# Hybrid decoder block: block sums and norm scales on one engine, another order of seven block products

## The chip, the cores and the metric

The kernel runs on one core of one Trainium2 chip. The time is the device time of one execution in microseconds (us). Of several executions the median counts. The engines are TensorE (PE; its weight loads are PEld), VectorE (DVE), ScalarE (ACT), GpSimd (POOL) and SyncE (SP). SP and POOL also start DMAs; each does what it is given in order.

## The reference

One decoder block, 1024 tokens, width 1024, float32. The part around the change, cut:

```
h = rms_norm(x, norm1_g)
z = h @ w_in                      # (1024, 3352 + 2048): q 512 | kv 768 | gates 24 | retention 2048 | merge 2048
q = rms_norm(zq per head of 64) * nsa_q_norm              # 8 heads
k_slc, k_win = rms_norm(k per head of 64) * nsa_k_norm[1], [2]     # 2 groups each
v_slc, v_win                                              # as they are
y_nsa = gates * (compressed, selected, sliding-window attention over q, k, v)
y_ret = silu(g) * group_norm(retention(q, k, v))
x = x + (sigmoid(zm) * (y_nsa @ w_b0, y_ret @ w_b1)).sum() @ w_out
x = x + (silu(rms_norm(x) @ w_gate) * (rms_norm(x) @ w_up)) @ w_down
```

## The kernel before

A float32 product is made of three fp32r products: each operand is split into a high part (a ScalarE copy to fp32r) and a low part (a VectorE subtraction). The normed input lies transposed in `H` as such a pair.

The kernel is written as generators that yield operations (`Op`), allocations (`Alloc`) and waits on flags (`Wait`). A planner, `Sched`, picks the next operation by costs of its own, and the order of picking is the order on each engine. `Any` gives it two engines to choose from, one VectorE, one GpSimd. A `Ring` or `Bag` is a set of buffers. What the planner's time says is not what the chip does; the chip waits on semaphores, each engine in its own order.

The change lies in the stage between the input norm and the retention projections, some 50 to 220 us into the span. It computes the 512 columns of q and 512 columns of k and v (branches 1 and 2) for all tokens as a 2 by 2 block product with seven multiplications instead of eight. Tokens 0 to 511 and 512 to 1023 are the two row blocks, the two halves of the width are the inner blocks, q and kv the column blocks.

- `g_sums` makes the sums of activation blocks out of `H` (11 VectorE subtractions and additions for each of four k), splits two of them into `gSa` and `gSb`, and stores two others in `s_scr`, which `s_back` loads back later and splits into `gSa` and `gSb` when products 6 and 7 have read these. Its scratch tiles come from `gt_ring`, three tiles of 128x512 (later five).
- The weight blocks are loaded into `R[0]` to `R[3]` by `b_loads`, 128x512 for each k. `R[1]` and `R[3]` serve other ends before that (compressed keys, gate values).
- `qk_sums` makes the sums of weight blocks in place in `R` and in tiles of `gt_ring`; `sub` lets the planner choose VectorE or GpSimd.
- `qk_ops` and `qk_fill` split each weight operand into one of six `oq` tiles, in the order of `QSEQ`.
- `qk_main` is the TensorE side: for each product p and token tile t, 12 matmuls (4 k, 3 parts). Products 1, 6, 7 and 4 add up in four banks (psS, psO); 2, 5 and 3 take a psF bank each. `qk_post` reads them out: product 2 gives q tiles 0 to 3, product 5 gives k/v tiles 4 to 7, product 3 k/v tiles 0 to 3, product 4 q tiles 4 to 7.
- `q_tile` and `kv_tile` norm a tile: square (ACT), sum (DVE), power −1/2 (POOL, `rsq`), scale (DVE), multiplication by `gq` or `gk` (POOL), split into `cat` (ACT, DVE), transposes (PE, psT), copy to a tile of `gt_ring` (ACT), DMA to `q_scr`, `k_scr`, `v_scr`. There are two `cat` tiles.
- `g_main` follows with the retention projections by the same seven-product scheme: products (1,0), (2,0), (1,1), (2,1) need only `H` and raw weights, then come those with `gRS` (sums from `sp_scr`, loaded by POOL's DMA into the space of `R`), whose weight sums (`gTab`) take the space of `cat`.

L316 is the matmul, L320 and L321 transposes, L336 a ScalarE copy, L346 a VectorE or GpSimd two-operand operation, L365 the sum, L386 and L387 the two GpSimd steps of `rsq`, L369 a DMA from POOL, L370 one from SP.

Of the kernel before, what the change touches and what calls it, by code (L numbers as in the profile page):

```python
# [9 lines left out]
F32 = mybir.dt.float32  # L10
# [250 lines left out]
def kernel(  # L261
# [144 lines left out]
        return bass.AP(tensor=ap.tensor, offset=ap.offset, ap=[[0, 128], [1, n]])  # L406

    q_scr = [[dram.tile([192, 512], F32, name=f"q_scr{g}_{t}") for t in range(NT)] for g in range(2)]
    k_scr = [dram.tile([128, 2, T], F32, name=f"k_scr{br}") for br in range(2)]
    v_scr = [dram.tile([128, 2, NT, 128], F32, name=f"v_scr{br}") for br in range(2)]  # L410
    r_scr = [[dram.tile([128, T], F32, name=f"r_scr{h}_{i}") for i in range(4)] for h in range(4)]
    s_scr = [dram.tile([128, 4, 512], F32, name=f"s_scr{i}") for i in range(2)]
    sp_scr = [dram.tile([128, 2, 4, 512], F32, name=f"sp_scr{i}") for i in range(2)]
# [120 lines left out]
    def a_loads():  # L534
        yield from x_load(0)
        yield dma(grow, norm1_g)
        for kk in range(4):
            yield from w_load(kk)
            if kk == 1:
                yield from x_load(1)  # L540
        yield dma(rawZ, w_cols(G0, 0, 8, 24))
        sch.spawn(a_wsplit(whA[:, 0, :, 256:280], whA[:, 1, :, 256:280], rawZ, 4), 3)
        for t in range(2, NT):
            yield from x_load(t)
        for i in range(3):
            yield dma(gk[:, i, :], bcast_rows(nsa_k_norm[0, i], HD))
        yield dma(q1, bcast_rows(nsa_q_norm[0], HD))
        yield Op("dve", 70, 60, [zpad], [], lambda: dve.memset(zpad, 0.0))
        yield dma(c_scr[:, :, T:T + 16, :].rearrange("a g t d -> t (a g) d"), zpad)
        yield from load_units(z_units[:2])  # L550
        yield from cw_loads()
        yield Wait(lambda: all(("xn", t) in fl for t in range(NT)))
        sch.spawn(split_units(z_units), 3)
        yield from load_units(z_units[2:3])
        yield Wait(lambda: ("cX", 1) in fl)
        yield from load_units(z_units[3:])
        for m, k in ((0, 0), (2, 1), (1, 2)):
            yield Wait(lambda: ("ss", 1, k) in fl)
            yield from b_loads((m,))
        yield Wait(lambda: "plain" in fl)  # L560
        yield from b_loads((3,))
        for j, S in ((2, gSa), (3, gSb)):
            for k in range(4):
                yield Wait(lambda: ("gS", j, k) in fl)
                yield dma(sp_scr[j - 2][:, :, k], S[:, :, k].bitcast(F32))
# [167 lines left out]
    def q_tile(t, z, free):  # L733
        zv = z.rearrange("p (h d) -> p h d", d=HD)
        own = yield Alloc(gt_ring)
        qn = own.rearrange("p (h d) -> p h d", d=HD)
        yield from q_norm(zv, qn, qn)
        free()
        yield tt(qn, qn, qk["gq"], ALU.mult, gp)
        cat = yield Alloc(qk["cat"])  # L740
        yield from split(cat[:, :, 0:64], cat[:, :, 64:128], qn)
        gt_ring.release(own)
        for g in range(2):
            tp = yield Alloc(t_ring)
# [12 lines left out]
    def kv_tile(t, z, free):
        zv = z.rearrange("p (b c n) -> p b c n", b=2, c=2)
        kz, vz = [zv[:, :, i].rearrange("p b (g d) -> p b g d", g=2) for i in range(2)]
        vs = yield Alloc(gt_ring)  # L760
        vw = vs.bitcast(F32R).rearrange("p (b g n) -> p b g n", b=2, g=2)
        yield from split(vw[:, :, :, 0:64], vw[:, :, :, 64:128], vz)
        for b in range(2):
            yield dma(v_scr[b][:, :, t, :], vs[:, b * 256:b * 256 + 256].rearrange("p (g n) -> p g n", g=2))
        gt_ring.release(vs)
        yield from q_norm(kz, vz, kz)
        yield tt(kz, kz, gk[:, 1:3, None, :].to_broadcast([128, 2, 2, HD]), ALU.mult, gp)
        cat = yield Alloc(qk["cat"])
        cv = cat[:, 0:4].rearrange("p (b g) n -> p b g n", b=2)
        yield from split(cv[:, :, :, 0:64], cv[:, :, :, 64:128], kz)  # L770
        free()
        tp = yield Alloc(t_ring)
        for j in range(4):
            yield tr(tp[:, j * 128:(j + 1) * 128], cat[:, j, :])
        qk["cat"].release(cat)
        ks = yield Alloc(gt_ring)
        yield ac(ks.bitcast(F32R), tp)
        t_ring.release(tp)
        for b in range(2):
            yield dma(k_scr[b][:, :, t * 128:(t + 1) * 128], ks[:, b * 256:b * 256 + 256].rearrange("p (g n) -> p g n", g=2))  # L780
            fl.add(("kv", b, t))
        gt_ring.release(ks)
        fl.add(("post", "k", t))

# [57 lines left out]
    gps = ExitStack()  # L842
    gtp, gpr, gpq = [gps.enter_context(tc.tile_pool(name=n, bufs=1, side="right")) for n in ("gtp", "gpr", "gpq")]
    gm, gops, gT1, gT2, gT4, gt, qk = {}, {}, {}, {}, {}, {}, {}
    gt_ring = Bag([gtp.tile([128, 512], F32, name=f"gt{n}") for n in range(3)])
    gSb = gpr.tile([128, 2, 4, 512], F32R, name="gSb")
    gSa = gpq.tile([128, 2, 4, 512], F32R, name="gSa")
    cp = ExitStack()
# [48 lines left out]
    def g_sums():  # L897
        yield Wait(lambda: ("cX", 1) in fl)
        def w(v):
            return v.rearrange("p (t n) -> p t n", t=4)  # L900

        def put(j, k, v):
            S = gSa if j == 2 else gSb
            yield from split(S[:, 0, k], S[:, 1, k], v)
            fl.add(("gS", j, k))

        for k in range(4):
            def h(i, j, p):
                return H[:, p, 4 * i:4 * i + 4, 4 * j + k, :].bitcast(F32)
            a = yield Alloc(gt_ring)  # L910
            yield tt(w(a), h(1, 0, 0), h(1, 1, 0), ALU.add)
            t = yield Alloc(gt_ring)
            yield tt(w(t), h(1, 0, 1), h(1, 1, 1), ALU.add)
            yield tt(a, a, t, ALU.add)
            yield tt(w(t), w(a), h(0, 0, 0), ALU.subtract)
            yield dma(s_scr[0][:, k], a, lat=2000)
            fl.add(("ss", 0, k))
            gt_ring.release(a)
            yield tt(w(t), w(t), h(0, 0, 1), ALU.subtract)
            yield from put(2, k, t)  # L920
            s = yield Alloc(gt_ring)
            yield tt(w(s), h(1, 1, 0), w(t), ALU.subtract)
            yield tt(w(s), w(s), h(1, 1, 1), ALU.add)
            yield from put(3, k, s)
            gt_ring.release(s)
            yield tt(w(t), h(0, 1, 0), w(t), ALU.subtract)
            yield tt(w(t), w(t), h(0, 1, 1), ALU.add)
            yield dma(s_scr[1][:, k], t, lat=2000)
            fl.add(("ss", 1, k))
            gt_ring.release(t)  # L930
        fl.add("gS0")

    def s_back():
# [11 lines left out]
        for t in raws:  # L945
            raw_ring.release(t)
        fl.add("back")
        for j, b, after in ((2, 1, 7), (2, 0, 5), (3, 1, 3), (3, 0, 4)):
            yield Wait(lambda: all((after, k) in q_ops for k in range(4)))
            S = gm["S", j, b] = gl.tile([128, 4, 512], F32R, name="gRS", tag=f"r{j * 2 - 4 + b}")  # L950
            yield dma(S, sp_scr[j - 2][:, b], gp)

    QSEQ = (1, 2, 6, 7, 5, 3, 4)
    q_ops = {}

    def qk_ops():
# [22 lines left out]
    def qk_sums(odd):  # L979
# [115 lines left out]
    def g_loads():  # L1095
        yield Wait(lambda: "back" in fl)
        gm["raw"] = [(yield Alloc(raw_ring)), (yield Alloc(raw_ring))]
        for j, (n, f) in enumerate(g_todo):
            if j == 2:
                yield Wait(lambda: ("P", 4) in fl)  # L1100
                gm["raw"] += [gpl.tile([128, 8, 128], F32, name="xx", tag=f"o{i}") for i in (2, 3)]
            h, i = r_pairs[f]
            t = yield Alloc(graw_ring)
            yield dma(t, r_units[h][i + (n == "U")].src)
            gm[n, f] = t
# [16 lines left out]
    def g_ops():  # L1122
        gm["h"] = []
        made = set()
        for n, (p, f) in enumerate(gseq):
            yield Wait(lambda: ("G", f) in gm)
            G = gm["G", f]
            if n < 4:
                yield Wait(lambda: all((4, k) in q_ops for k in range(4)) and (4, 5, 0, 1)[n] not in qk["op"].held)
            if n in (4, 6):  # L1130
                yield Wait(lambda: "wh" in fl)
                gm["h"].append((yield Alloc(hl_ring)))
# [72 lines left out]
        gop_ring.release(w)  # L1205

    def g_main():
        yield Wait(lambda: "plain" in fl and ("P", 4) in fl)
        Y, Z = {}, {}
        for p, f in gseq:  # L1210
            yield Wait(lambda: (p, f) in gops and (p not in (6, 7) or all(("S", p - 4, b) in gm for b in range(2))))
# [477 lines left out]
    def load_group(g):  # L1689
        yield Wait(lambda: us[0] in qt)  # L1690
        for br in (1, 0):
            kT[br].append(kvp.tile([128, T], F32R, name=f"kT{br}"))
            vv[br].append(kvp.tile([128, NT, 128], F32R, name=f"vv{br}"))
            yield dma(kT[br][g], k_scr[br][:, g], gp, 3000)
            yield dma(vv[br][g], v_scr[br][:, g], gp, 3000)
            fl.add("kv1")
        fl.add(("gkv", g))

# [816 lines left out]
```

## Time and profile before

| | us |
|---|---|
| median of 3 runs | 1583.86 |
| lowest, highest | 1582.41, 1584.09 |
| profiled execution | 1583.02 |
| its span | 1581.2 |
| TensorE busy | 1544.2 |
| VectorE busy | 1063.3 |
| ScalarE busy | 754.3 |
| GpSimd busy | 310.4 |

Each row of the timeline has the start in us, the time from the first start to the last end of a merged run of equal instructions, the engine, the line, the operation with output and inputs, a count, and in brackets the idle time before it with what ended it. A row of the windows has the stretch, its length, then for PE, PEld, DVE, ACT, POOL the busy time and the number of instructions, TensorE's granted clock, the share of the DMA engines and GB/s. A row of the groups has busy time, mean ns of one, and the idle time before.

### The profile page before, as it was taken

What the parts mean: (1) busy time and instruction counts of PE and PEld (TensorE: products, weight loads), DVE (VectorE), ACT (ScalarE), POOL (GpSimd) and SP (SyncE); (2) the same over time, 40 slices, a digit from 0 to 9 for tenths busy, and PEclk for the clock granted to TensorE, in tenths of its full rate; (3) what the DMA queues carried; (4) which work ended last, traced back from release to release, by engine and by line L of the source; (5) the groups of instructions that cost most, each with busy time, mean ns of one, the idle gap of its engine ahead of it and who ended that gap; (6) DMA issues with size and microseconds to landing.
All of it is one profiled execution on the core that took longest, in us unless ns stands there. A gap on an engine that the chain in (4) does not pass through costs nothing.

```text
span 1581.2 us, 22432 instructions
## 1 busy us (share of the span) xinstructions
PE 1544.2 (98%) x7869; PEld 1305.9 (83%) x7869; DVE 1063.3 (67%) x2203; ACT 754.3 (48%) x1533; POOL 310.4 (20%) x398
## 2 busy tenths in 40 slices
PE   9999889999999999999999999999999999999999
PEld 8877678888899898898878787888888888788887
DVE  7587775544788866789848459566665655477674
ACT  6235553335777667667614326333333333344442
POOL 3034430002232210322000101332343332000000
PEclk9999989999999999999999999999999999999999
DMA  7674754326433345127375323444444434397521
GB/s 225 177 226 161 213 180 126 114 87 200 134 90 94 105 141 160 62 86 218 122 279 178 119 96 98 163 136 142 149 146 146 161 133 147 136 400 250 181 73 54
DMA packets 194451, 241.41 MB, mean 153 GB/s; under 512 B 22177, under 2 KB 121505, under 8 KB 193570
## 3 DMA queue, kind: packets, MB, share of 16 engines
q1 hardware_dynamic: 181282, 198.03, 38.6%
q0 software_dynamic: 13056, 41.95, 8.1%
q8 instruction: 62, 1.02, 0.3%
q14 instruction: 51, 0.42, 0.1%
HBM read 163.37 MB, written 76.56 MB: 152 GB/s over the span
## 4 chain that ended last, share of the span: by engine, by line
PE 74%; DVE 5%; DMA 3%; ACT 1%; issue 1%; SPq 1%; POOL 0%; DVEq 0%; POOLq 0%; ACTq 0%
PE psS L316 24%; PE psF L316 23%; PE psO L316 12%; PE psT L316 11%; PE psT L321 4%; DMA mx<-u_scr 1%; DMA qt<-q_scr 1%; SPq L370 1%; DMA yraw<-y_scr 1%; DVE H L346 1%; PE psF L321 0%; DVE pT L346 0%; DVE wh L346 0%; DVE P L1492 0%; DVE sh L346 0%
## 5 line engine op out<-in xcount | busy, mean ns | idle before, releaser
L316 PE MATMUL psF<-H,wh 128*128 128x512 f32 x804 | 210.0, 396 | 1.9 <-ACT aw L336 1.9
L316 PEld LDWEIGHTS psF<-H,wh 128*128 128x128 f32 x804 | 146.8, 188 | 28.0 <-ACT aw L336 2.7
L316 PE MATMUL psS<-H,wh 128*128 128x512 f32 x576 | 157.0, 399 | 1.9 <-DVE sgm L356 1.3
L316 PEld LDWEIGHTS psS<-H,wh 128*128 128x128 f32 x576 | 104.2, 188 | 19.9 <-DVE sgm L356 1.8
L336 ACT ACTIVATE P<-P,pm 128x640 f32<-128x640 f32 (+7 forms) x128 | 94.0, 735 | 45.5 <-DVE pm L1492 43.2
L346 DVE TENSOR_TENSOR pT<-psT,pT 128x512 fp32r<-128x512 f32 (+1 forms) x152 | 91.8, 615 | 32.6 <-ACT pT L336 32.1
L316 PE MATMUL psS<-kT,qt 128*128 128x384 f32 (+3 forms) x384 | 101.8, 344 | 0.1
L336 ACT ACTIVATE pT<-psT 128x512 fp32r<-128x512 f32 (+1 forms) x152 | 77.8, 535 | 44.9 <-PE psT L321 44.6
L316 PE MATMUL psO<-pT,vv 128*128 128x256 f32 x528 | 91.7, 291 | 2.2 <-DVE pT L346 2.2
L316 PEld LDWEIGHTS psO<-pT,vv 128*128 128x128 f32 x528 | 78.7, 189 | 11.3 <-DVE pT L346 4.7
L321 PE MATMUL psT<-ident,P 128*128 128x128 f32 x528 | 77.3, 273 | 0.6 <-DVE pT L346 0.6
L316 PEld LDWEIGHTS psS<-kT,qt 128*128 128x128 f32 x384 | 64.8, 189 | 7.4 <-DVE pm L1492 0.9
L346 DVE TENSOR_TENSOR wh<-wraw,wh 128x512 fp32r<-128x512 f32 (+1 forms) x53 | 51.1, 971 | 25.4 <-ACT wh L336 25.4
L321 PEld LDWEIGHTS psT<-ident,P 128*128 128x128 f32 x528 | 61.1, 140 | 4.5 <-DVE pT L346 1.3
L336 ACT ACTIVATE op<-T 128x512 fp32r<-128x512 f32 x55 | 34.6, 630 | 61.6 <-PE psT L316 34.1
L336 ACT ACTIVATE wh<-wraw 128x512 fp32r<-128x512 f32 (+1 forms) x54 | 43.6, 815 | 33.8 <-DMA mx<-u_scr 9.9
L316 PE MATMUL psS<-wo,H 128*128 128x512 f32 x216 | 59.0, 393 | 0.5 <-DVE sgm L356 0.5
L369 POOL DMA_DIRECT2D qt<-q_scr x16 | 12.5, 779 | 237.8 <-PE psF L316 153.1
L346 DVE TENSOR_TENSOR op<-T,op 128x512 fp32r<-128x512 f32 x55 | 47.9, 875 | 14.9 <-ACT op L336 13.9
L316 PE MATMUL psS<-op 128*128 128x512 f32 x234 | 57.6, 389 | 0.0
L386 POOL TENSOR_SCALAR rs<-ss 128x1 f32<-128x1 f32 x17 | 6.0, 355 | 249.3 <-ACT hx L336 199.2
L316 PE MATMUL psF<-H,op 128*128 128x512 f32 x228 | 54.0, 389 | 0.0
(562 smaller groups left out, 3721.6 us busy)
## 6 DMA issues: line engine op xcount, KB each, us to landing
wraw<-in_w_in_dram SPq DMA_DIRECT2D x24, 512.0 KB, 4.2
row<-in_ffn_w_down_dram POOLq DMA_DIRECT2D x22, 512.0 KB, 5.6
f_scr<-fs SPq DMA_DIRECT2D x22, 512.0 KB, 2.6
t_scr<-row POOLq DMA_DIRECT2D x22, 512.0 KB, 3.0
qt<-q_scr POOLq DMA_DIRECT2D x16, 512.0 KB, 4.2
st<-t_scr SPq DMA_DIRECT2D x31, 256.0 KB, 4.8
z_scr<-zs SPq DMA_DIRECT2D x24, 256.0 KB, 2.7
wraw<-in_ffn_w_gate_dram SPq DMA_DIRECT2D x12, 512.0 KB, 3.7
```

The source lines that it names most:

```text
L316: lambda: pe.matmul(o, l, r, start=start, stop=stop, skip_group_check=True))
L321: return Op("pe", 109, 100, [o], [i], lambda: pe.transpose(o, i, ident))
L336: return Op("act", c, 150, outs, ins, lambda: act.activation(o, i, func, scale=scale, **kw))
L346: return vop(o, [a, b], lambda: (eng or dve).tensor_tensor(o, a, b, op), eng)
L369: r = Op("gp", 1040, lat, [o], [i], lambda: gp.dma_start(o, i)) if eng is gp else \
L370: Op("sp", 50, lat, [o], [i], lambda: sp.dma_start(o, i))
L386: lambda: gp.tensor_scalar(dst, v, eps, None, op0=ALU.add))
```

## The change

Four things. `sub` no longer offers GpSimd, and the multiplications by `gq` and `gk` move from GpSimd to VectorE. `g_sums` takes its tiles from a ring of its own, the three `gt` tiles and the four slices of `R[2]`; the `gt` tiles go over to `gt_ring` when the sums are done, and the weight blocks are loaded in the order 0, 1, 2, 3, each one k of the sums later. The order of the block products is 1 2 6 7 4 5 3 and the flags that name a product follow. Keys and values of a tile go out in one DMA each, into one `k_scr` and one `v_scr`.

```diff
-    k_scr = [dram.tile([128, 2, T], F32, name=f"k_scr{br}") for br in range(2)]
-    v_scr = [dram.tile([128, 2, NT, 128], F32, name=f"v_scr{br}") for br in range(2)]
+    k_scr = dram.tile([128, 4, T], F32, name="k_scr")
+    v_scr = dram.tile([128, 4, NT, 128], F32, name="v_scr")
...
-        for m, k in ((0, 0), (2, 1), (1, 2)):
+        for m, k in ((0, 1), (1, 2), (2, 3)):
             yield Wait(lambda: ("ss", 1, k) in fl)
             yield from b_loads((m,))
...
-        yield tt(qn, qn, qk["gq"], ALU.mult, gp)
+        yield tt(qn, qn, qk["gq"], ALU.mult)
...
-        for b in range(2):
-            yield dma(v_scr[b][:, :, t, :], vs[:, b * 256:b * 256 + 256].rearrange("p (g n) -> p g n", g=2))
+        yield dma(v_scr[:, :, t, :], vs.rearrange("p (a n) -> p a n", a=4))
...
-        yield tt(kz, kz, gk[:, 1:3, None, :].to_broadcast([128, 2, 2, HD]), ALU.mult, gp)
+        yield tt(kz, kz, gk[:, 1:3, None, :].to_broadcast([128, 2, 2, HD]), ALU.mult)
...
-        for b in range(2):
-            yield dma(k_scr[b][:, :, t * 128:(t + 1) * 128], ks[:, b * 256:b * 256 + 256].rearrange("p (g n) -> p g n", g=2))
-            fl.add(("kv", b, t))
+        yield dma(k_scr[:, :, t * 128:(t + 1) * 128], ks.rearrange("p (a n) -> p a n", a=4))
+        fl.update((("kv", 0, t), ("kv", 1, t)))
...
-    gt_ring = Bag([gtp.tile([128, 512], F32, name=f"gt{n}") for n in range(3)])
+    gts = [gtp.tile([128, 512], F32, name=f"gt{n}") for n in range(3)]
+    sm_ring = Bag(gts + [R[2][:, k] for k in range(4)])
+    gt_ring = Bag([])
...
-            a = yield Alloc(gt_ring)
+            a = yield Alloc(sm_ring)
...
+        gt_ring.tiles.extend(gts)
         fl.add("gS0")
...
-        for j, b, after in ((2, 1, 7), (2, 0, 5), (3, 1, 3), (3, 0, 4)):
+        for j, b, after in ((2, 1, 7), (3, 0, 4), (2, 0, 5), (3, 1, 3)):
...
-    QSEQ = (1, 2, 6, 7, 5, 3, 4)
+    QSEQ = (1, 2, 6, 7, 4, 5, 3)
...
         def sub(o, a, b):
-            return Any(tt(o, a, b, ALU.subtract), tt(o, a, b, ALU.subtract, gp))
+            return tt(o, a, b, ALU.subtract)
...
-                yield Wait(lambda: ("P", 4) in fl)
+                yield Wait(lambda: ("P", 3) in fl)
...
-            yield dma(kT[br][g], k_scr[br][:, g], gp, 3000)
-            yield dma(vv[br][g], v_scr[br][:, g], gp, 3000)
+            yield dma(kT[br][g], k_scr[:, 2 * br + g], gp, 3000)
+            yield dma(vv[br][g], v_scr[:, 2 * br + g], gp, 3000)
```

How this moves instructions, at three places. First VectorE, from the first splits of product 1's operands on (`oq<-gR`; `gt` tiles with `H` are activation sums, `gR` and `ga` without `oq` are weight sums). Before:

```order
L346 TENSOR_TENSOR oq<-gR,oq 128x512 x6
L346 TENSOR_TENSOR gt_729<-gt_729,H 128x512
L346 TENSOR_TENSOR gSa<-gt_729,gSa 128x512
L346 TENSOR_TENSOR gt_730<-H,gt_729 128x512
L346 TENSOR_TENSOR gt_730<-gt_730,H 128x512
L346 TENSOR_TENSOR ga_1168<-gR 128x512
L346 TENSOR_TENSOR gR<-gR 128x512
L346 TENSOR_TENSOR ga_1169<-gR 128x512
L346 TENSOR_TENSOR gSb<-gt_730,gSb 128x512
L346 TENSOR_TENSOR gt_729<-H,gt_729 128x512
L346 TENSOR_TENSOR gt_729<-gt_729,H 128x512
L346 TENSOR_TENSOR oq<-gR,oq 128x512 x2
```

And in the changed kernel:

```order
L346 TENSOR_TENSOR oq<-gR,oq 128x512 x4
L346 TENSOR_TENSOR gSb<-gR,gSb 128x512
L346 TENSOR_TENSOR gR<-H,gR 128x512
L346 TENSOR_TENSOR gR<-gR,H 128x512
L346 TENSOR_TENSOR gR<-gR 128x512 x2
L346 TENSOR_TENSOR oq<-gR,oq 128x512 x2
L346 TENSOR_TENSOR ga_1168<-gR 128x512
L346 TENSOR_TENSOR gR<-gR 128x512
L346 TENSOR_TENSOR oq<-gR,oq 128x512
L346 TENSOR_TENSOR ga_1169<-gR 128x512
L346 TENSOR_TENSOR gR<-gR 128x512
L346 TENSOR_TENSOR oq<-gR,oq 128x512
```

Three activation sums stand behind the first splits where seven stood, and the last two operands of product 2 stand behind weight sums that read `R[3]`.

Second SP's DMA starts at the end of the activation sums (`gR<-in_w_in_dram` are the weight blocks, `wraw<-s_scr` the loads back). Before:

```order
L370 DMA s_scr_123<-gt_730 128x512
L370 DMA gR<-in_w_in_dram 128x512 x4
L370 DMA z_scr_0_1059<-gR 128x512
L370 DMA s_scr_122<-gt_731 128x512
L370 DMA z_scr_0_1059<-gR 128x512
L370 DMA gR<-in_w_in_dram 128x512 x4
L370 DMA sp_scr_124<-gSa 256x1x512 x3
L370 DMA wraw<-s_scr_122 128x512 x4
```

And in the changed kernel:

```order
L370 DMA s_scr_121<-gt_729 128x512
L370 DMA gR<-in_w_in_dram 128x512 x4
L370 DMA s_scr_120<-gt_728 128x512
L370 DMA z_scr_0_1058<-gR 128x512
L370 DMA wraw<-s_scr_120 128x512 x4
L370 DMA z_scr_0_1058<-gR 128x512
L370 DMA s_scr_121<-gR 128x512
L370 DMA gR<-in_w_in_dram 128x512 x8
L370 DMA sp_scr_122<-gSa 256x1x512 x4
```

Two weight blocks, `R[2]` and `R[3]`, are loaded together behind the last `s_scr` write; before, `R[3]` was loaded last and alone.

Third TensorE at the end of product 7 (`psO<-oq,gSb`), with the transposes of normed tiles (`psT<-identr,cat`) between. Before:

```order
L320 MATMUL psT<-identr,cat 128x128 x4
L316 MATMUL psS<-oq,gSb 128x512 x19
L316 MATMUL psO<-oq,gSb 128x512 x12
L316 MATMUL psF<-oq,gSa 128x512 x48
L316 MATMUL psF<-oq,gSb 128x512 x12
L320 MATMUL psT<-identr,cat 128x128 x4
L316 MATMUL psF<-oq,gSb 128x512 x7
```

And in the changed kernel:

```order
L320 MATMUL psT<-identr,cat 128x128 x4
L316 MATMUL psS<-oq,gSb 128x512
L316 MATMUL psO<-oq,gSb 128x512 x12
L316 MATMUL psS<-oq,H 128x512 x36
L316 MATMUL psO<-oq,H 128x512 x12
L320 MATMUL psT<-identr,cat 128x128 x4
L316 MATMUL psF<-oq,gSa 128x512 x7
```

Product 4, which reads `H`, now stands between product 7 and products 5 and 3.

More of the change, by code (lines that the diff above doesn't have):

```diff
@@ L909, in h @@
                 return H[:, p, 4 * i:4 * i + 4, 4 * j + k, :].bitcast(F32)
-            a = yield Alloc(gt_ring)
+            a = yield Alloc(sm_ring)
             yield tt(w(a), h(1, 0, 0), h(1, 1, 0), ALU.add)
-            t = yield Alloc(gt_ring)
+            t = yield Alloc(sm_ring)
             yield tt(w(t), h(1, 0, 1), h(1, 1, 1), ALU.add)
@@ L917, in g_sums @@
             fl.add(("ss", 0, k))
-            gt_ring.release(a)
+            sm_ring.release(a)
             yield tt(w(t), w(t), h(0, 0, 1), ALU.subtract)
             yield from put(2, k, t)
-            s = yield Alloc(gt_ring)
+            s = yield Alloc(sm_ring)
             yield tt(w(s), h(1, 1, 0), w(t), ALU.subtract)
@@ L924, in g_sums @@
             yield from put(3, k, s)
-            gt_ring.release(s)
+            sm_ring.release(s)
             yield tt(w(t), h(0, 1, 0), w(t), ALU.subtract)
@@ L929, in g_sums @@
             fl.add(("ss", 1, k))
-            gt_ring.release(t)
+            sm_ring.release(t)
+        gt_ring.tiles.extend(gts)
         fl.add("gS0")
@@ L1128, in g_ops @@
             if n < 4:
-                yield Wait(lambda: all((4, k) in q_ops for k in range(4)) and (4, 5, 0, 1)[n] not in qk["op"].held)
+                yield Wait(lambda: all((3, k) in q_ops for k in range(4)) and (4, 5, 0, 1)[n] not in qk["op"].held)
             if n in (4, 6):
@@ L1207, in g_main @@
     def g_main():
-        yield Wait(lambda: "plain" in fl and ("P", 4) in fl)
+        yield Wait(lambda: "plain" in fl and ("P", 3) in fl)
         Y, Z = {}, {}
```

## The prediction

> **What bounds the kernel now.** The first view is the page's busy line, the second the table of windows that I cut at the starts of the block products.
>
> ```profile
> PE 1544.2 (98%) x7869; PEld 1305.9 (83%) x7869; DVE 1063.3 (67%) x2203; ACT 754.3 (48%) x1533; POOL 310.4 (20%) x398
> ...
> 58.00:102.00 44.00, 44.00 (x245) 37.60 (x244) 31.66 (x67) 12.81 (x27) 2.31 (x3) 1.00 0.58 177
> 102.00:113.00 11.00, 11.00 (x51) 9.09 (x50) 10.27 (x11) 5.46 (x10) 9.25 (x5) 1.00 0.86 275
> 113.00:129.00 16.00, 12.69 (x49) 9.98 (x48) 13.67 (x18) 4.21 (x8) 10.32 (x9) 0.89 0.66 238
> 129.00:157.50 28.50, 25.69 (x130) 20.46 (x129) 19.69 (x24) 18.15 (x34) 11.74 (x10) 1.00 0.50 156
> 157.50:185.30 27.80, 24.25 (x113) 19.08 (x113) 23.88 (x45) 14.58 (x33) 11.67 (x17) 1.00 0.68 210
> 185.30:201.70 16.40, 13.90 (x62) 11.14 (x61) 11.18 (x21) 8.18 (x18) 10.54 (x14) 0.90 0.69 186
> 201.70:222.00 20.30, 15.91 (x86) 12.38 (x84) 12.88 (x17) 11.88 (x22) 9.39 (x9) 0.91 0.73 228
> 222.00:340.00 118.00, 117.98 (x514) 97.62 (x515) 63.11 (x96) 43.30 (x74) 0.00 (x0) 0.99 0.40 118
> ```
>
> TensorE bounds the whole, and whatever leaves its busy time alone costs nothing. Before 102 and after 222 it has no gap here; between them it idles 16.6 us (16.0 − 12.69, 28.5 − 25.69, 27.8 − 24.25, 16.4 − 13.90, 20.3 − 15.91), and in three windows its clock is at 0.89 to 0.91. The edits move instructions only between 50 and 222 us; from the gRS products on every engine's order reads as before. So the answer lies in this stretch. Third view, TensorE's timeline there:
>
> ```profile
> 102.09 8.32 PE L316 MATMUL psS<-oq,H 128*128 128x512 f32 x36
> 118.03 11.23 PE L316 MATMUL psF<-oq,H 128*128 128x512 f32 x41 [3.31 <-DVE oq L346]
> 129.10 2.43 PE L316 MATMUL psS<-oq,gSa 128*128 128x512 f32 x10
> 157.55 5.60 PE L316 MATMUL psF<-oq,gSa 128*128 128x512 f32 x24
> 174.36 0.51 PE L320 MATMUL psT<-identr,cat 128*128 128x128 f32 x4 [2.00 <-DVE cat L346]
> 196.53 0.51 PE L320 MATMUL psT<-identr,cat 128*128 128x128 f32 x4 [2.50 <-DVE cat L346]
> 197.72 4.11 PE L316 MATMUL psO<-oq,H 128*128 128x512 f32 x10
> 201.67 2.89 PE L316 MATMUL psS<-H,oq 128*128 128x512 f32 x12
> 205.31 0.46 PE L320 MATMUL psT<-identr,cat 128*128 128x128 f32 x4
> 205.61 1.85 PE L316 MATMUL psT<-H,oq 128*128 128x512 f32 x7
> 216.24 1.74 PE L320 MATMUL psT<-identr,cat 128*128 128x128 f32 x12
> 222.02 6.89 PE L316 MATMUL psS<-gRS,wh 128*128 128x512 f32 x23 [1.08 <-DVE wh L346]
> 228.75 2.88 PE L316 MATMUL psF<-gSa,wh 128*128 128x512 f32 x12
> 231.47 2.88 PE L316 MATMUL psS<-gRS,wh 128*128 128x512 f32 x12
> ```
>
> Twelve matmuls cost 2.72 (228.75 to 231.47), four transposes 0.30 (205.31 to 205.61). From 102.09 to 228.75 stand 28 groups of twelve for the seven block products, 4 of the first w_in products, 2 with gRS, and 24 sets of transposes: 34 × 2.72 + 24 × 0.30 = 99.7 us. The row takes 126.7, so 27.0 are lost, waits and slow clock together. By stage: products 1 and 2 (102.09 to 129.10, 8 groups) 5.2; 6 and 7 (to 157.55, 8 groups, 8 sets) 4.3; 5, 3 and 4 (to 201.67, 12 groups, 7 sets) 9.4; the tail to 228.75 (6 groups, 9 sets) 8.1. These 27.0 are all that can be won. All waits name VectorE or what it feeds, so the fourth view is its timeline beside GpSimd's, and the groups by form:
>
> ```profile
> 56.92 0.68 DVE L346 TENSOR_TENSOR gt<-H,gt 128x512 f32<-128x512 f32 x1
> 100.01 3.69 DVE L346 TENSOR_TENSOR oq<-gR,oq 128x512 fp32r<-128x512 f32 x6
> 105.94 1.77 DVE L346 TENSOR_TENSOR gt<-H,gt 128x512 f32<-128x512 f32 x1
> 127.92 0.69 DVE L346 TENSOR_TENSOR oq<-gt,oq 128x512 fp32r<-128x512 f32 x1 [0.65 <-ACT oq L336]
> 128.53 1.79 DVE L346 TENSOR_TENSOR gR<-gR,gt 128x512 f32<-128x512 f32 x1
> 210.54 1.16 DVE L346 TENSOR_TENSOR cat<-wh,cat 128x256 fp32r<-128x256 f32 x1 [0.91 <-ACT cat L336]
> ...
> 126.83 1.69 POOL L387 TENSOR_TENSOR rsq<-rsq,half 128x8 f32<-128x8 f32 x1
> 128.48 1.30 POOL L346 TENSOR_TENSOR ga<-ga,gq 128x512 f32<-128x512 f32 x1
> ...
> L387 POOL TENSOR_TENSOR rsq<-rsq,half 128x4 f32<-128x4 f32 x8 | 8.3, 1037 | 0.4
> L365 DVE TENSOR_REDUCE ssq<-wh 128x4 f32<-128x256 f32 x8 | 3.2, 412 | 0.6 <-ACT wh L336 0.6
> ```
>
> The same form, H and gt to gt, takes 0.68 with GpSimd idle and 1.77 at 105.94. An operand pair both in SBUF is held up while GpSimd runs a 128x512 or 128x256 operation (128.53 beside 128.48); the small rsq power at 126.83 doesn't hold up 127.92. Nineteen VectorE rows in the stretch, from that of 105.94 to that of 210.54, are long in this way, together 17.2 us over their usual 0.68 or 0.41.
>
> The Trainium skill, "SBUF — State Buffer", section "SBUF: two separate sides", has a rule for this: VectorE with two SBUF inputs and GpSimd lock one port pair, each for a whole instruction. The long rows agree. The power at 126.83 does not: by the letter of the rule it would have held up 127.92.
>
> **The change part by part.** The 25 GpSimd operations (9 block sums, 8 multiplications by gq, 8 by gk) go to VectorE: 17 × 0.61 (127.92 to 128.53) + 8 × 0.34 (estimate: 0.41 less the same overlap of 0.07) = 13.1 us of work added; 17.2 us of hold-up leave, since GpSimd keeps only the rsq pairs and DMA starts. VectorE's busy time in the stretch falls by 4.1, and what matters more, each link in a chain costs 0.6 and not 1.3 to 1.8.
>
> The sums of the activations get four more buffers. VectorE then has three of their 44 instructions left behind the start of the oq splits, where it had seven: 4 × 0.61 = 2.4 us out of the chain to product 2. Ahead of that TensorE has no gap, and the added rows fall in VectorE's idle time before the cXT rows (31.66 busy of 44.00): nothing. But the buffers are R[2], so the R[2] loads wait for the last sum:
>
> ```profile
> 79.75 1.88 SPq L370 DMA_DIRECT2D gR<-in_w_in_dram  x4
> 103.30 2.04 SPq L370 DMA_DIRECT2D gR<-in_w_in_dram  x4
> 117.41 0.35 SPq L370 DMA_DIRECT2D s_scr<-gt x1
> ...
> DMA to landing us min/median/max: 1.9/4.2/11.1
> s_scr<-gt SPq DMA_DIRECT2D x1, 256.0 KB, 2.5
> ```
>
> The R[2] loads of 79.75 move behind the last s_scr write, and the R[3] loads of 103.30 behind them. VectorE is at the oq splits at 100.0, as in the row of 100.01, since as many rows stand ahead of them; four splits, one gSb split and two sums at 0.61 to 0.7 end at 104.4, and the write goes out there rather than at 117.41. Two R[2] loads follow; the third must wait until that write has read its slice, 2.5 later (the s_scr row), 107.5. Six loads then go out 0.45 apart and land about 4.2 later (the gR landing row): R[2] complete by 112.2, first R[3] by 112.7. VectorE waits there for R[3], for a sum that now stands ahead of product 2's last two splits: the third operand is split two steps behind it, 114.5, the fourth three further, 116.4. Product 2 is due at 112.97 (four groups behind 102.09) and at 0.68 an operand stops 0.2 for the third and 1.3 for the fourth, then 0.9 for a psF bank, because the first eviction now stands behind six more rows. Lost: 2.4 against 5.2 now, of which 3.31 is the wait and 1.8 the slow clock behind it (41 matmuls, 11.07 to the next row against 9.29). Bounds of the load term: 1.9 landing gives no wait, 11.1 gives 7 more.
>
> Products 6 and 7: carried on so, 0.61 a row in the new order, product 6 starts at 126.3, its last operand is split by 127.6 and due at 128.3; the first cat is there by 135.0 and due at 135.3. This is tight, so I take 1.0 lost of 4.3.
>
> Products 4, 5, 3. Product 4 reads H and operands made early. It stands where product 5 was, and gives tile 4's rsq chain 10.9 us of cover. The 2.00 at 174.36 was the first k tile, whose chain ran through GpSimd and slow rows beside product 3. The 2.50 at 196.53 has another root:
>
> ```profile
> 194.00 0.60 ACT L336 ACTIVATE ga<-psS 128x512 f32<-128x512 f32 x1 [5.53 <-DMA k_scr<-ga]
> ```
>
> ScalarE stood 5.53 for a buffer that a k_scr write still read, and the cat behind it was late. In the new order the q tiles take their buffers before the k tiles do. With rows at their short length I find every operand 0.2 to 2 us early; for what such a walk misses on three in-order engines I take 2.0 lost of 9.4. The bounds are 0.3 and, if all cat waits return, 6. The slow clock after 196.53 (10 matmuls from 197.72 to 201.67, 3.95 against 2.27) goes with its wait. The skill's "TensorE: Matmul & The Clock Gate", section "What's actually happening", gives an idle window of about 3.4 us for a lower clock; here 2.50 was followed by one. By the page only the wait of 3.31 would come near it, and 1.7 of this gain would be put down to something else.
>
> The tail. After product 3 seven k tiles are still to be transposed, beside 4 groups: 10.9 + 2.1 = 13.0 us of cover. Then the gTab sums need the cat space: from the last transposes' end (217.98) to the full stream at 222.02 it is 4.0, plus 1.5 slow clock (23 matmuls, 6.73 against 5.21); both stay. I take 7.5 lost of 8.1.
>
> One write a tile for keys and values, 16 SP starts fewer: nothing, no engine waits for SP's issue. The wait on k_scr above could grow with a 256 KB write, which is part of the 2.0.
>
> Sum: 2.8 + 3.3 + 7.4 + 0.6 = 14.1 off. The profiled execution took 1583.02 (span 1581.2), 0.8 under the median of 1583.86 and inside 1582.41 to 1584.09: 1583.0 − 14.1 = 1568.9, said as 1569. Nothing behind 222 gives it back, since TensorE is 117.98 busy of the next 118.00.
>
> **The rivals.**
> - Late loads. R[2] and R[3] land at the long end, 11.1. Product 2 loses 7 more and some clock: 14.1 − 8 gives 1577. For it: eight loads start within 5 us. Against: sp_scr's writes now come behind them. Chance 0.12.
> - The tail grows: slower. All k tiles now come last, with two cat buffers. A tile's chain is about 4.8 (estimate: seven steps of 0.41 as in the ssq row, 1.28 of rsq, less overlaps, a 0.46 transpose). One after another, 7 × 4.8 = 33.6 against 13.0 of cover: 20.6 more, 1569 + 20.6 = 1589.6. Two at a time it is 19.2, 6.2 more, 1575. It decides above 27 us for seven tiles (13.0 + 14.1). Against: rows of several tiles alternate in VectorE's new order. Chance 0.07 slower, and 0.08 that it eats the gain to within 0.2%.
> - VectorE becomes the bound, because the long rows are not GpSimd's doing. Then 13.1 are added, and four sums fewer at 1.7 save 6.8: 6.3 more on the chain, 1589. Against: 56.92 and 105.94. Chance 0.02, and I count it with slower.
> - The port rule by its letter, as a mechanism: each of the 16 rsq powers (8.3 for eight) stops two-SBUF rows, of which there are 25 more. At 20% of the stretch and 0.8 each, 4 us of hold-up, 1573. The skill's page above would have it so. Row 127.92 speaks against. Chance 0.05.
> - More than forecast: none of my allowances is needed, 1563 or less. Chance 0.08.
>
> **How the numbers follow.** Forecast 1564 to 1573 with 0.58. About 0.2% (3.2 us) is what a measurement can tell from no change. Faster: 0.58 + 0.12 + 0.05 + 0.08 = 0.83; same 0.08; slower 0.09. The range that leaves two in ten out goes from 1563 to 1578, up to the late loads.
>
> **What would show it.** In the changed profile: no VectorE 128x512 row over 0.75 between 100 and 200 us; product 6 begins near 126 (129.10 now); the last of products 5, 3, 4 ends near 187 (201.67 now); the gRS stream begins near 207 (222.02 now). The forecast is wrong if product 2 waits over 5 us on oq, if the transposes wait on cat by over 6 us in sum, or if over 22 us lie between product 3's end and the gRS stream.

## The result, and the profile after

The changed kernel takes 1568.54 us in the median of 5 runs (1567.61 to 1570.28), the kernel before 1583.30 in 5 (1582.32 to 1584.09): ratio 0.9908, 95% interval 0.9893 to 0.9922. It is 14.8 us faster; 1569 was forecast. The profiled execution took 1568.88, its span is 1567.2. The page's busy line:

```profile
PE 1541.0 (98%) x7869; PEld 1304.9 (83%) x7869; DVE 1058.5 (68%) x2228; ACT 752.1 (48%) x1533; POOL 282.0 (18%) x373
```

VectorE has 25 instructions more and is busy 4.8 us less. The next view is the table of windows, of before and then of after, each cut at the same three places: the four products 1, 2, 6, 7; the three products 4, 5, 3 in their order; the tail up to the second matmul group with gRS.

```profile
102.09:157.55 55.46, 49.34 (x225) 39.50 (x224) 43.58 (x51) 27.78 (x50) 31.21 (x22) 0.97 0.62 203
157.55:201.67 44.12, 38.08 (x174) 30.17 (x173) 34.98 (x65) 22.71 (x50) 22.17 (x31) 0.96 0.69 201
201.67:228.75 27.08, 22.67 (x109) 17.88 (x108) 19.61 (x28) 15.45 (x27) 9.42 (x9) 0.87 0.78 236
```

```profile
100.97:149.99 49.02, 47.47 (x226) 38.40 (x224) 36.61 (x60) 27.00 (x49) 11.82 (x8) 1.00 0.63 208
149.99:187.53 37.54, 36.56 (x181) 30.01 (x180) 31.75 (x60) 20.93 (x45) 19.16 (x22) 1.00 0.85 269
187.53:215.05 27.52, 23.11 (x101) 17.88 (x100) 21.07 (x44) 15.30 (x32) 5.14 (x7) 0.88 0.84 249
```

The four products take 6.4 us less, the three 6.6 less, the tail 0.4 more: 12.6 in all. Of the span's 14.0 another 1.1 is already there at 101, and it is no work of the change: the first 24 transposes of the program took 5.32 us in the one execution and 4.29 in the other (in the profiled executions of all runs below the stage starts between 100.5 and 102.3). The last 0.3 lies behind the stage. TensorE's timeline of after, the starts of the parts and the waits that are left:

```profile
100.97 8.32 PE L316 MATMUL psS<-oq,H 128*128 128x512 f32 x36
114.70 3.47 PE L316 MATMUL psF<-oq,H 128*128 128x512 f32 x14 [0.42 <-DVE oq L346]
118.91 5.73 PE L316 MATMUL psF<-oq,H 128*128 128x512 f32 x24 [0.75 <-DVE wh L346]
124.48 8.32 PE L316 MATMUL psS<-oq,gSa 128*128 128x512 f32 x36
134.09 0.54 PE L320 MATMUL psT<-identr,cat 128*128 128x128 f32 x4 [0.38 <-DVE cat L346]
149.99 8.32 PE L316 MATMUL psS<-oq,H 128*128 128x512 f32 x36
177.64 2.13 PE L316 MATMUL psF<-oq,gSb 128*128 128x512 f32 x8 [0.71 <-DVE wh L346]
187.53 2.43 PE L316 MATMUL psS<-H,oq 128*128 128x512 f32 x10
191.74 0.51 PE L320 MATMUL psT<-identr,cat 128*128 128x128 f32 x4 [0.94 <-DVE cat L346]
199.30 2.12 PE L316 MATMUL psT<-H,oq 128*128 128x512 f32 x8 [0.58 <-ACT ga L336]
203.83 0.54 PE L320 MATMUL psT<-identr,cat 128*128 128x128 f32 x4 [0.81 <-DVE cat L346]
205.89 0.80 PE L316 MATMUL psS<-gRS,wh 128*128 128x512 f32 x1 [1.52 <-ACT wh L336]
207.16 8.06 PE L316 MATMUL psS<-gRS,wh 128*128 128x512 f32 x23 [0.47 <-DVE wh L346]
215.05 2.88 PE L316 MATMUL psF<-gSa,wh 128*128 128x512 f32 x12
```

The waits of 3.31, 2.00 and 2.50 are gone. Most of what is left stands in the tail (4.3 of 6.6 us by these rows), and with it a slow clock: the 23 matmuls from 207.16 take 7.89 to the next row, at a granted clock of 0.65.

### The profile page after: what moved, and what is told of

It reads as the page before. It is cut to its first block, busy times and chain, and to the rows that moved or that the text cites. A ratio compares the mean times of both kernels' runs of the same rounds, so it can differ in the third digit from the quotient of the medians.

```text
span 1567.2 us, 22380 instructions
## 1 busy us (share of the span) xinstructions
PE 1541.0 (98%) x7869; PEld 1304.9 (83%) x7869; DVE 1058.5 (68%) x2228; ACT 752.1 (48%) x1533; POOL 282.0 (18%) x373
## 4 chain that ended last, share of the span: by engine, by line
PE 80%; DVE 6%; DMA 4%; ACT 2%; issue 1%; POOL 1%; SPq 0%; ACTq 0%; DVEq 0%; POOLq 0%
PE psS L316 27%; PE psF L316 23%; PE psO L316 13%; PE psT L316 12%; PE psT L321 4%; DMA q_scr<-gt 1%; DMA sgm<-z_scr 1%; DVE H L346 1%; PE psF L321 0%; SPq L370 0%; DVE P L1493 0%; DVE wh L346 0%; DMA sg<-z_scr 0%; DMA yraw<-y_scr 0%; DVE gR L346 0%
## 5 line engine op out<-in xcount | busy, mean ns | idle before, releaser
L316 PEld LDWEIGHTS psF<-H,wh 128*128 128x128 f32 x804 | 146.8, 188 | 28.1 <-ACT aw L336 2.7
L346 DVE TENSOR_TENSOR op<-T,op 128x512 fp32r<-128x512 f32 x55 | 49.6, 905 | 15.3 <-ACT op L336 14.4
L316 PE MATMUL psF<-sh,op 128*128 128x512 f32 x216 | 52.1, 390 | 1.2 <-DVE sh L346 1.2
```

What stands on the lines that cost most here:

```text
L316: lambda: pe.matmul(o, l, r, start=start, stop=stop, skip_group_check=True))
L346: return vop(o, [a, b], lambda: (eng or dve).tensor_tensor(o, a, b, op), eng)
```

## The experiments

The table puts the runs together: the median, the ratio to the kernel before in the same session with its interval, and the three parts of the stage in the profiled execution, cut as above. The medians of before in the experiments' sessions lay between 1583.6 and 1584.6. "Other books" means that the planner reckons the 25 moved operations as GpSimd's and orders by that, while they are issued on VectorE.

| run | median | ratio | four products | three products | tail |
|---|---|---|---|---|---|
| before | 1583.30 | | 55.5 | 44.1 | 27.1 |
| changed kernel | 1568.54 | 0.9908 (0.9893–0.9922) | 49.0 | 37.5 | 27.5 |
| engines alone | 1580.36 | 0.9977 (0.9968–0.9986) | 58.7 | 37.3 | 25.7 |
| order alone | 1573.40 | 0.9938 (0.9924–0.9952) | 55.4 | 38.5 | 24.0 |
| ring alone | 1582.76 | 0.9988 (0.9979–0.9997) | 55.5 | 42.4 | 28.9 |
| one write alone | 1582.58 | 0.9991 (0.9982–1.0000) | 55.5 | 45.4 | 27.5 |
| all but engines | 1569.66 | 0.9909 (0.9896–0.9923) | 55.3 | 39.2 | 19.9 |
| all but order | 1569.84 | 0.9910 (0.9897–0.9924) | 49.4 | 35.8 | 29.5 |
| all but ring | 1578.81 | 0.9970 (0.9959–0.9981) | 59.0 | 39.3 | 24.7 |
| engines, orders of before | 1578.93 | 0.9968 (0.9955–0.9980) | 50.8 | 44.0 | 28.1 |
| the same, with unused GpSimd copies | 1594.26 | 1.0058 (1.0044–1.0072) | 62.4 | 45.6 | 31.3 |
| engines and order, other books | 1570.63 | 0.9915 (0.9900–0.9929) | 51.3 | 39.5 | 23.5 |
| changed kernel, other books | 1566.38 | 0.9883 (0.9867–0.9900) | 51.6 | 39.4 | 19.6 |
| changed kernel, short q write | 1565.86 | 0.9887 (0.9872–0.9902) | 49.3 | 36.2 | 25.9 |

**Each edit alone.** The theory was that of the prediction: GpSimd's operations hold up VectorE, and most of the gain is the engines'.

Engines alone (`sub` gives only `tt(o, a, b, ALU.subtract)`, and the multiplications by gq and gk lose `gp`):

> The kernel before with the first edit alone: block sums and the gq and gk multiplications on VectorE only; ring, order and writes as before. Theory (GpSimd's 128x512 and 128x256 operations hold up VectorE's two-operand SBUF rows, and each link of the chains runs there): no VectorE 128x512 row above 0.75 us between 100 and 200, and most of the 14 us comes from this edit, 8 to 11 us: 1572 to 1575. What stays is the wait on the k_scr buffer before product 4 and its clock, about 4. Rival (order and buffers carry the gain, the engine edit only swaps one cost for another): within 3 us of before, 1580 to 1586. Rival (VectorE becomes the bound, 13 us of work on its chain): 1589.

It came to 4.1 us: half of the least that the theory wanted, and inside the rival's 1580 to 1586. The window table has 58.7 for the four products, 3.2 more than before, and the timeline shows why:

```profile
130.50 1.25 PE L320 MATMUL psT<-identr,cat 128*128 128x128 f32 x8 [6.62 <-DVE cat L346]
```

Product 2 has almost no wait (0.19). But the planner, which reckons VectorE as fuller now, has put 16 transposes of q tiles ahead of product 6's first matmul, and TensorE stands 6.62 us for the first of them. So this run doesn't tell what the engines are worth; that takes a run with the orders held.

Order alone:

```diff
-    QSEQ = (1, 2, 6, 7, 5, 3, 4)
+    QSEQ = (1, 2, 6, 7, 4, 5, 3)
```

> The kernel before with the order 1 2 6 7 4 5 3 alone. Theory: the 5.53 us wait of ScalarE on the k_scr buffer and the 2.50 wait of TensorE behind it go (about 4 with the slow clock), but the kv chains, with long rows and a GpSimd multiplication in each, now come last and the tail grows by 2 to 4: 1579 to 1584. Rival (the order carries the gain): 1573 to 1576, with the tail no longer than before.

11.0 us: the rival's size. The three products take 38.5 instead of 44.1 and the tail got shorter, with all of GpSimd's operations in place.

Ring alone (seven tiles for `g_sums`, weight loads one k later), and one write alone (`k_scr` and `v_scr` as one tensor each):

> The kernel before with the seven tiles for the activation sums and the later weight loads alone. Theory: at most the 2.4 us of rows taken from behind the first splits, and the block sums on GpSimd still hold VectorE up: 1580 to 1584. Rival (the ring carries the gain of products 1 and 2, 3.5): 1579 or less, and product 6 begins near 125.6. Rival (loads late): 1587 or more, TensorE waits over 5 us on operands of product 2.

> The kernel before with one write a tile for keys and values alone. Theory: nothing, 1581 to 1585, since no engine waits for SP's issue; the buffer waits on k_scr and v_scr stay within 1 us of what they were. Rival (two writes a tile held the buffer twice as long): the 5.53 us wait on k_scr falls below 4 and 1 to 3 us are won, 1580 to 1582.

Both are 1.7 to 1.8 us under the session's median of before. Their stages took 126.8 and 128.4 us against 126.7, so no gain stands in the stage; where the 1.7 to 1.8 come from isn't settled. In the run with one write the wait on a k_scr buffer is gone, but ScalarE waits 2.65 for a v_scr buffer instead, and TensorE still 2.10 for cat.

**All but one.**

> The changed kernel with the old order 1 2 6 7 5 3 4. Theory (engines and order remove the same loss in products 5, 3, 4, so that the order adds little once the engines are changed): first half as in the changed kernel, second half as with the engines alone, 49.0 + 37.3 + 25.7 = 112 us for the stage against 114.1: 1566 to 1570. Rival (the order carries 11 us in any surroundings, as it did alone): 1577 to 1581.

> The changed kernel with block sums and the gq and gk multiplications back on GpSimd. Theory: the first half loses again what it lost before (products 1, 2, 6, 7 take 55 us, not 49), the second half is that of the order alone: 1572 to 1575. Rival (ring and one write help beside the order): 1569 to 1571.

> The changed kernel with the old three-tile ring and the old order of the weight loads. Its TensorE order again has 16 transposes ahead of product 6's matmuls. Theory (the ring's part is that it lets the planner put product 6 first): TensorE idles over 5 us ahead of product 6, products 1, 2, 6, 7 take 58 us, and the rest is as in the changed kernel: 1576 to 1579. Rival (the ring is worth what it gave alone, under 2): 1568 to 1571.

Beside the other three, the order looks worthless (1569.84 without it, 1568.54 with it), and so do the engines (1569.66). But these kernels spend their time in different places. Without the engines the four products take 55.3, as the theory said, but the time is the rival's, by a tail of 19.9 that neither expected. Without the ring the 16 transposes ahead of product 6 are back, with the same 6.62 us, and 10 us are lost, as expected. Alone the ring moved the four products by nothing (55.47); its part is that with the engines changed the planner then puts product 6 first.

**The engines with every order held.** The planner goes on reckoning the 25 operations as GpSimd's, but they are issued on VectorE:

```diff
+    def vgp(o, a, b, op):
+        return vop(o, [a, b], lambda: dve.tensor_tensor(o, a, b, op), gp)
...
-            return Any(tt(o, a, b, ALU.subtract), tt(o, a, b, ALU.subtract, gp))
+            return Any(tt(o, a, b, ALU.subtract), vgp(o, a, b, ALU.subtract))
```

(and the same for gq and gk).

> The 25 operations are issued on VectorE, but the planner goes on reckoning as if 9 block sums and the gq and gk multiplications were GpSimd's, so every other engine's order is word for word that of before. It tells the engine edit from the new order of transposes that came with it in the run with the engine edit alone (16 transposes ahead of product 6, TensorE 6.62 us idle there). Theory (the hold-up by GpSimd costs 12 to 13 us, and the 8 us lost at product 6 were the order): 1571 to 1574, product 6 begins within 22.5 us of product 1, products 5, 3, 4 lose 2 to 3. Rival (the chains are no shorter on VectorE, the gain of 4 is all that the engines give): 1579 to 1582.

The time is near the rival's, 4.7 us off, and the windows say where:

```profile
101.87:152.70 50.83, 47.54 (x226) 38.37 (x224) 39.72 (x64) 27.27 (x50) 9.84 (x9) 1.00 0.67 223
152.70:196.74 44.04, 38.03 (x174) 30.08 (x172) 32.72 (x70) 22.55 (x50) 15.31 (x23) 0.96 0.67 194
```

The four products win 4.6, as the theory has it. One link can be followed: the split that product 2 waited 3.31 us for before, there and in this run.

```profile
117.30 1.28 DVE L346 TENSOR_TENSOR oq<-gR,oq 128x512 fp32r<-128x512 f32 x2
```

```profile
112.27 1.28 DVE L346 TENSOR_TENSOR oq<-gR,oq 128x512 fp32r<-128x512 f32 x2
```

Counted from the start of product 1 it came at 15.21 and comes at 10.40, though VectorE has three more rows ahead of it. Six rows there (105.94 to 115.74) were 6.3 us over their usual length. The wait of 3.31 is gone.

The three products win nothing (44.04 for 44.12), though no VectorE row there is long any more. Of the first k tile's 2.00 a wait of 1.42 stays, and the one ahead of product 4's end is 2.73 instead of 2.50:

```profile
169.24 0.51 PE L320 MATMUL psT<-identr,cat 128*128 128x128 f32 x4 [1.42 <-DVE cat L346]
193.16 0.51 PE L320 MATMUL psT<-identr,cat 128*128 128x128 f32 x4 [2.73 <-DVE cat L346]
```

The root of the second can be read from when DMAs land. First before: GpSimd's start of the last gRS load, SP's starts of a k tile's writes, then the two with their size and their median time to landing, and behind them the k tile's writes that started at 179.90 (the ScalarE row at 194.00 stands in the prediction). Then this run, in which `vgp` moves the lines by three:

```profile
186.00 0.64 POOL L369 DMA_DIRECT2D gRS<-sp_scr  x1 [3.05 <-DVE oq L346]
186.41 1.23 SPq L370 DMA_DIRECT2D k_scr<-ga  x2
...
gRS<-sp_scr POOLq DMA_DIRECT2D x1, 1024.0 KB, 7.2
k_scr<-ga SPq DMA_DIRECT2D x2, 128.0 KB, 7.0
...
k_scr<-ga SPq DMA_DIRECT2D x2, 128.0 KB, 2.2
```

```profile
182.06 0.61 POOL L372 DMA_DIRECT2D gRS<-sp_scr  x1 [6.01 <-DVE oq L346]
182.47 1.23 SPq L373 DMA_DIRECT2D k_scr<-ga  x2
190.44 0.60 ACT L336 ACTIVATE ga<-psS 128x512 f32<-128x512 f32 x1 [5.79 <-PE psS L316]
```

The k tile's writes start 0.41 us behind a load of 1 MB. They land about 7 us later, just behind the load (193.23), where the same writes took 2.2 shortly before. The second lands at 193.89, and ScalarE goes on at 194.00. With the ring alone the load starts at 185.81, the writes 0.41 later, the second lands at 193.60, and ScalarE goes on at 193.71; in this run it lands at 190.33, and ScalarE goes on at 190.44, though the row names PE (a matmul run happens to end at 190.43). It is 0.11 us each time. In the run with one write a tile the v_scr write that ScalarE waits 2.65 us for starts 0.4 us behind the load too. So it is not GpSimd's arithmetic that costs this wait. It hangs on where the load and the writes stand in the orders; that the load is the cause is read from the traces, and no run moved the load alone. With the order 4 5 3 alone, and with the engines alone, TensorE has no wait over 0.6 in the three products.

**Is it the hold-up, or only the shorter operations?** Moving an operation takes GpSimd's load away and also makes that link shorter. So another run keeps the moved operations and adds behind each a GpSimd copy, GpSimd's queue being that of before word for word:

```diff
+            dve.tensor_tensor(o, a, b, op)
...
+            gp.tensor_tensor(d, o, b if b.shape == o.shape and b.tensor.name != o.tensor.name else o, op)
```

> The run with the 25 operations on VectorE and all orders of before, and behind each of the 25 a GpSimd operation of the same shape on the same data, whose result (written over the window mask, so the attention's output is not the reference's) nobody in this stage uses. GpSimd's queue is that of before word for word. Theory (GpSimd's operations hold VectorE up, and this costs the 4.6 us of products 1, 2, 6, 7): VectorE 128x512 rows of 1.3 to 1.8 are back, this part takes 53 to 56 us instead of 50.8, 1581 to 1586. Rival (the 4.6 came from shorter links: a sum or multiplication of 0.68 on VectorE instead of 1.3 to 1.8 on GpSimd, and held-up rows had slack): long rows are back but the part takes 51.5 or less, 1578 to 1580.

15.3 us more than without the copies (14.4, when each is set against the kernel before in its own session), and 12 of them in the four products (62.42 for 50.83). No engine waits for a copy by the table of waits. But VectorE's rows are long again: in its timeline from 99 to 242 I count 20 of them, 14.7 us over their usual 0.68 or 0.42. The place ahead of product 2's second half, on VectorE (L350 is the moved operation), GpSimd (L356 is the copy) and TensorE:

```profile
117.56 1.67 DVE L350 TENSOR_TENSOR gt<-gR 128x512 f32<-128x512 f32 x1
119.15 1.52 DVE L346 TENSOR_TENSOR gR<-gR 128x512 f32<-128x512 f32 x1
120.60 1.74 DVE L346 TENSOR_TENSOR oq<-ga,oq 128x512 fp32r<-128x512 f32 x1
125.74 0.68 DVE L346 TENSOR_TENSOR wh<-psF,wh 128x512 f32<-128x512 f32 x1
...
120.20 1.59 POOL L356 TENSOR_TENSOR Mw<-gt,gR 128x512 f32<-128x512 f32 x1
...
126.47 7.35 PE L316 MATMUL psF<-oq,H 128*128 128x512 f32 x24 [7.15 <-DVE wh L346]
```

The eviction of psF (125.74), for which TensorE waits, stands behind these rows. Six long rows ahead of it are 5.5 us over their usual length together, and counted from the start of product 1 it comes 5.6 us later than without the copies. So the hold-up is shown, with a price: 14 to 15 us for 25 GpSimd operations whose results nobody waits for. Not all of it is held-up rows: in the tail a power step of `rsq` (217.92) stands behind two copies in GpSimd's queue, and VectorE waits 2.25 us for it. And the part took more than the 53 to 56 us of the theory, for VectorE now has the 25 operations and the hold-up at once; so the run doesn't say how much of the 4.6 us is hold-up and how much is shorter links.

**The tail.** The run with all but the engines had a tail of 19.9. Was that its order, or its slower first half that gave the k chains time? The changed kernel with the planner's books as there, and the operations on VectorE (`vgp` as above):

> The changed kernel, all 25 operations on VectorE, but with the instruction orders of the run that had all but the engine edit (the planner reckons the 25 as GpSimd's). That run took 55.3 us for products 1, 2, 6, 7 and 59.1 from product 4 to the full gRS stream; the changed kernel took 49.0 and 65.1. Theory (the first half is the engines', the tail of the changed kernel is an order of instructions that its planner chose): first half 50 to 51.5, second half 58 to 60, 1562 to 1565, the fastest so far. Rival (what the first half wins, the tail must give back, since the k chains there are bound by themselves): second half 63 or more, 1567 to 1570.

```profile
192.13:211.73 19.60, 19.21 (x97) 15.22 (x96) 16.25 (x34) 12.11 (x26) 3.04 (x4) 1.00 0.85 249
...
206.38 5.51 PE L316 MATMUL psS<-gRS,wh 128*128 128x512 f32 x23 [0.39 <-DVE wh L346]
```

The tail is short again with the operations on VectorE and the orders of that run: it was the order. Ten sets of transposes stand between the matmuls of products 5 and 3 and six behind, where the changed kernel has nine and seven; nothing waits over 0.4 in the tail, and the same 23 matmuls take 5.35 to the next row at full clock. The stage is 3.5 us shorter than in the changed kernel (110.6 for 114.1), the time about 2 (1563.71 to 1566.72 against 1567.61 to 1570.28; the two ratios' intervals overlap a little), and the median lies between the two expectations: in the profiled executions 1.1 is given back behind the stage, for which the cause stays open. It is the fastest of the kernels that leave nothing out. The same books without ring and single writes:

> The kernel before with the order 1 2 6 7 4 5 3 and the 25 operations on VectorE, the planner reckoning them as GpSimd's: no ring, no single writes, TensorE's order that of the run with the order alone. Theory (ring and writes give nothing of their own; the 10 us that the changed kernel lost without its ring were the 16 transposes that the planner then put ahead of product 6): first half 50 to 51, second half 61 to 63, 1568 to 1571. Rival (the ring's tiles and later loads are what the engines need): 1576 or more.

1570.63, as the theory had it: the ring isn't needed for the first half. It takes 3.9 us more in the tail than with ring and single writes; which of the two helps there was not taken apart.

Four rows of the table now tell the two large edits apart, for in them the planner's books stay those of before: before, engines with the orders of before, order alone, and this run. The four products take 55.5 and 55.4 with the 25 operations on GpSimd, 50.8 and 51.3 with them on VectorE, in either order. The three products take 44.1 and 44.0 in the old order, 38.5 and 39.5 in the new, on either engine.

At last the writes. Each q half goes to q_scr twice, the second time 64 rows; one row is left of these:

```diff
+            r.fn = lambda: sp.dma_start(q_scr[g][t][128:129], qs[0:1])
```

> The changed kernel, all orders unchanged; the second write of each q half to q_scr (64 rows, 128 KB, a copy of the first 64) writes one row only, and the loads of queries read the first half twice, so the attention's queries are not the reference's. It takes 2 MB of writes out of the stage. Theory (the DMA engines, 0.85 busy from product 4 on, hold the q_scr buffers, ScalarE waits 6.9 us for them between 171 and 187 and the k chains come late): these waits fall below 3, the tail of 27.5 below 25, 1563 to 1566. Rival (the tail hangs on the order and on two cat tiles): 1567 to 1570, the tail 27 or more.

The table of ScalarE's waits from 125 to 216, of the changed kernel and of this one:

```profile
ACT gt L336 <- DMA q_scr<-gt: 4.8, 3, 2.2
ACT ga L336 <- DMA q_scr<-ga: 2.8, 2, 2.1
```

```profile
ACT gt L336 <- DMA q_scr<-gt: 3.5, 2, 3.0
ACT ga L336 <- DMA q_scr<-ga: 0.5, 1, 0.5
```

7.6 us of waits become 4.0 (between 171 and 187 they fall from 6.9 to 3.5, not below 3), the three products and the tail 2.9 shorter together; the median is 2.7 under that of the changed kernel. In the changed kernel the four q_scr writes that ScalarE waits for between 171 and 187 start 0.4 to 2.7 us behind gRS loads (of 162.72 and 176.03) and land 6.5 to 8.7 us later, as the k tile's writes above. The tail of 25.9 lies between the two expectations: the buffers carry a part of it, and the order, by the run before, more.

## Why the prediction was right, and where its steps were not

The marks set beforehand came out: product 6 at 124.48 (near 126), the last of the three products' end at 187.53 (near 187), the gRS stream at 207.16 (near 207), no VectorE 128x512 row over 0.75. Three of them are places in time, and the stage's start, 1.1 us earlier, is in each; by the sum's own terms the end of the three products was due at 188.2 (201.67 − 2.8 − 3.3 − 7.4), and 187 was loosely said.

- Products 1, 2, 6, 7: 9.5 lost before, 3.4 forecast, 3.1 measured (49.02 − 16 × 2.72 − 8 × 0.30). Product 2 waits 0.42 for an operand and 0.75 for a bank (1.5 and 0.9 forecast). VectorE waits 1.80 us for R[3], until 110.94 (112.7 forecast). The cause holds: the engines bring 4.6 with all orders held, and unused copies on GpSimd cost 12. The 2.4 us that the ring was to take out of the chain to product 2 do not show in the run with the ring alone (55.5 for 55.5).
- Products 5, 3, 4: 2.0 lost was forecast, 2.2 measured (37.54 − 12 × 2.72 − 9 × 0.30). The size was right, and of the two causes one: the buffer that a k_scr write still read, and that another order frees. What kept that write so long was, by the traces, the load started ahead of it, which the prediction did not look at. The other cause was wrong. The step that put the 2.00 at 174.36 down to GpSimd and slow rows fails: at short rows and the old order 1.42 of it stays, and this part takes 44.04. Its gain is that of a new order, and each of two edits brings one by itself.
- The tail was mis-sized: 7.5 lost forecast, 9.1 measured (27.52 − 6 × 2.72 − 7 × 0.30). Its waits sum to 4.3 (0.94, 0.58, 0.81, 1.52, 0.47), where those of before summed to 4.1 (0.85, 2.17, 1.08), and the slow clock on the gRS stream is 2.7 (7.89 − 5.21), not 1.5. That costs 1.6, and the 1.1 of the program's start and 0.3 behind the stage, which have nothing to do with the change, made up for most of it. To that extent the hit on 1569 is luck.
- One write a tile, costed at nothing: no gain in the stage by its own run (128.4 for 126.7).
- What the prediction did not see is that the edits change each other's price through the planner. The engines are worth 4.1 alone, 4.7 with orders held, next to nothing beside the other three, and without the ring all the rest lose 10 us. It read the order that this one combination gives, and so its sum came out; the gains it put to the single edits did not.
- The rivals: late loads cost product 2 no more than the 0.42; the tail grew by 0.4 only (by 1.0, counted as loss, for two sets of transposes fewer stand in it); VectorE did not become the bound. The port rule by its letter did not show on VectorE, where no 128x512 row is long. One of the groups of after, with two operands in SBUF:

```profile
L346 DVE TENSOR_TENSOR gR<-gR 128x512 f32<-128x512 f32 x8 | 5.4, 682 | 0.0
```

## What to carry to other kernels

Where a planner sets the order, an edit has no price of its own: run it once with all orders held and once as planned, and cut the time at the same places in both. A long wait that a row puts down to one engine is checked by whether it moves with that engine's work; here one was named DMA in two runs and TensorE in a third, and in all three it ended 0.11 us after one write had landed. For a buffer that a DMA still reads, look at when the DMA lands and what large transfer started ahead of it, and not only at when it started. A 128x512 operation on GpSimd over SBUF operands isn't free when nobody waits for it, as long as VectorE is near the path.

## What the runs showed of the hardware

The hold-up goes the other way too. GpSimd's small first step of rsq takes 0.24 us beside VectorE rows with a single operand, as in the kernel before:

```profile
136.05 1.26 DVE L365 TENSOR_REDUCE ssq<-gt 128x8 f32<-128x512 f32 x2
...
136.81 0.24 POOL L386 TENSOR_SCALAR rsq<-ssq 128x8 f32<-128x8 f32 x1 [3.03 <-DVE ssq L365]
```

In the changed kernel, VectorE and GpSimd side by side:

```profile
128.97 0.68 DVE L346 TENSOR_TENSOR ga<-wh,rsq 128x512 f32<-128x512 f32 x1
129.57 0.68 DVE L346 TENSOR_TENSOR gt<-gt,gq 128x512 f32<-128x512 f32 x1
130.17 0.67 DVE L365 TENSOR_REDUCE ssq<-gt 128x8 f32<-128x512 f32 x1
...
128.00 2.34 POOL L386 TENSOR_SCALAR rsq<-ssq 128x8 f32<-128x8 f32 x1
...
125.97 0.67 DVE L365 TENSOR_REDUCE ssq<-ga 128x8 f32<-128x512 f32 x1
127.16 0.67 DVE L346 TENSOR_TENSOR gt<-wh,rsq 128x512 f32<-128x512 f32 x1
...
124.64 1.52 POOL L386 TENSOR_SCALAR rsq<-ssq 128x8 f32<-128x8 f32 x1
126.25 1.67 POOL L387 TENSOR_TENSOR rsq<-rsq,half 128x8 f32<-128x8 f32 x1
```

The step of 128.00 ends at 130.34, that of 124.64 at 126.16, each 0.2 us after VectorE's first row with a single operand (130.17, 125.97). Between rows with two SBUF operands back to back it found no gap. The long power step from 126.25 to 127.92 neither stretched nor held up the VectorE row at 127.16. So a small GpSimd operation in a chain costs up to ten times its own length beside a dense VectorE; here TensorE lost 0.38 by it at most, its only wait for cat in that part. The Trainium skill, "SBUF — State Buffer", section "SBUF: two separate sides", has one engine block the other for a whole instruction: the waiting small step agrees (2.34 for 0.24), the power step does not.
